# Tiles moved to 128-byte multiples, and another order of work between attention output and FFN, in a one-core diffusion layer

## The chip, the cores and the metric

The kernel runs on one core of a Trainium2 chip. The metric is the device time of one execution in microseconds (us). The core has five engines that work side by side from queues of their own: TensorE (PE in the profile; PEld is its loading of the standing operand), VectorE (DVE), ScalarE (ACT), GpSimd (POOL) and SyncE (SP), which here only issues transfers. A matmul multiplies a *standing* operand of 128 by 128, which is loaded first, with a *moving* operand of 128 partitions by up to 512 columns that streams past it; both are read from SBUF, the on-chip memory of 128 partitions, and the product goes to PSUM.

## The reference

One layer over 256 latent tokens with 256 context tokens, model width 2048, all in float32:

```python
h  = modulate(rms_norm(x, g_attn_pre), sh1, sc1)        # sh, sc, gt: six rows of silu(c) @ w_mod + b_mod
hc = modulate(rms_norm(ctx, g_attn_pre), csh1, csc1)
qa, ka, va, qb, kb, vb, ga, gb = split(h @ w_in)        # the same for hc: keys and values only
oa = window_gqa_latent(rope(qa), rope(ka), va, ka_c, va_c, sink_a)     # 8 heads, 2 key heads
ob = neighbourhood_latent(qb, kb, vb, kb_c, vb_c, rpb_b)               # 8 heads
y  = (sigmoid(ga) * (oa @ w_br_a) + sigmoid(gb) * (ob @ w_br_b)) @ w_o
x  = x + gt1 * rms_norm(y, g_attn_post)
h  = modulate(rms_norm(x, g_ffn_pre), sh2, sc2)
u  = depthwise_conv(h @ w_up)                           # 2 x 5632 channels, 3 taps over tokens
a, g = split(u)
x  = x + gt2 * rms_norm((silu(g) * a) @ w_down, g_ffn_post)
```

## The kernel before

**Arithmetic.** The large products are computed in float32r with both operands split in two: a rounded part (called wh for weights) and the rest (wl). Three products of the four are kept. A weight block is 128 x 2048 floats, 1 MB. `raw_block` loads it into one of four `raw` buffers, `halves` splits it: ACT copies raw to wh (L118), DVE writes raw minus wh to wl (L122), each in two pieces of 1024 columns. wh and wl have two buffers each in pool `wp`. Activations hold rounded part and rest side by side: `hx[:, k, 0]` and `hx[:, k, 1]`, 256 tokens each.

**Two patterns of matmul.** In the first, weights stand and activations move (`mm2`, L164 and L165): for each of the 16 slices of the width there is a pair, wh against 512 columns (rounded part and rest of the activations) and wl against 256 columns (rounded part alone). Queries (pq), gates (pg), branches (pb, moving tile `oab`) and the up projection (pu, moving tile `h2`) are made so. The keys (pk, L387) too, with 256 columns at a time. In the second, activations stand and weights move, in triples: (rounded, wh), (rest, wh), (rounded, wl). The values' projection V (pv, L585, standing `hx`, `hc`), the attention output Wo (py_o, L800, standing `zz`) and the down projection (py_d, L800, standing `ff`) are made so. Attention itself has scores (s, L681, standing q, moving k, 512 columns), transposes (L702) and values (po, L711, standing v, moving `pT`).

**Blocks and their order.** All weight blocks but the first ones stand in one list in order of use: V, queries, gates with branches, Wo (16 blocks), up (88), down (44). `block(ahead, split)` hands out the next one, splits the one after it if `split` is set, and loads `ahead` blocks beyond. The names `queue[...]` and `tc.issue_after(...)` tie a split or another operation to a place behind a given instruction of its engine. Outside one hand-ordered part at the start (keys), a planner orders each engine's queue by priority in the order of the program.

**Where tiles lie.** Pools are stacked from the left end of a partition (byte 16512, a multiple of 128) and from its right end (byte 229344, 96 more than a multiple of 128), in the order in which they are opened and their tiles made. In `cp`, the first tile is `col`, 2080 bytes long, so everything after it starts 32 bytes after a multiple of 128: `raw`, wh and wl too. Small tiles move the rest: hx, h2 and hc start at remainder 64, oab at 32, zz and ff at 96, q, k and v at 0, pT at 96.

**The passage.** `norm_gain` computes Wo (and later down) for 4 column slices of 512 and 2 halves of the tokens (t = 0 and 1). `close(t)` squares the finished slice on ACT with a sum (L805) and multiplies it by the gain row on DVE (L806). In the last slice the order changes: the last `lead` blocks (3 for Wo) are used for all of t = 0 first, then for t = 1, so that the first 128 tokens are done earlier. `done(t)` is here `residual(t)`: the inverse root of the mean square (`rstd_tok`, L836 to L839), the residual sum on DVE (L874) with squares on ACT (L877) for the second norm, its root; and after t = 1 the scaling of both halves (`scaled`, L890 on ACT, L892 on DVE, alternating). The last Wo block is split into buffers of its own in pool `yp` (`place`). The first up block is split between the two halves (`split_to(nblk[0])` after `done(0)`), behind the first residual slice (`queue[b0 + B_UP]`). Then 33 filler matmuls (`keep_busy`, L231) and the transposes of the 16 slices (L905) follow; from their result DVE and ACT make `h2`: a float32 copy h2t (L912 or L914), the rounded part h on ACT (L915), the rest on DVE (L916). With the first slices of h2 the up projection starts, four accumulators at once.

Of the kernel before, what the change touches and what calls it, by code (L numbers as in the profile page):

```python
# [58 lines left out]
def layer_kernel(ctx, tc, xc, xt, ccol, crow, wm_sc, wm_sd, wm_sh, wm_b, cols, wk, wkt, ws, rope, mask_a, bias_b, out):  # L59
# [6 lines left out]
    ps = ctx.enter_context(tc.tile_pool(name="ps", bufs=1, space=bass.MemoryType.PSUM))  # L66

    def acc(name):
        return ps.tile([P, 512], F32, tag="a", bufs=6, name=name)

    def bank(name):
        return ps.tile([P, 512], F32, tag="b", bufs=2, name=name)


    col = cp.tile([P, NCOL], F32, name="col")
    cc = cp.tile([P, KT, 32], F32, name="cc")
# [3 lines left out]
    gcol = cp.tile([P, 2, KT], F32, name="gcol")  # L80
    bgc = cp.tile([P, KT], F32, name="bgc")
    eps = cp.tile([P, 1], F32, name="eps")
    nc.gpsimd.memset(cc, 0.0)
# [6 lines left out]
        out=sel[:], in_=ident[:].rearrange("p (j w) -> p w j", j=4)[:, 0:2, :], axis=mybir.AxisListType.X, op=ALU.add)  # L90
    cr = cp.tile([2 * KT, P], F32, name="cr")
    c2 = cp.tile([P, KT, 2], F32, name="c2")
    nc.scalar.dma_start(out=c2, in_=ccol)
    nc.scalar.activation(cc[:, :, 0:2], c2[:], AF.Silu)

# [43 lines left out]
    raws, parts, nblk, place, queue, last = {}, {q: None for q in range(b0)}, [b0], {}, {}, []  # L139

    def load_to(i):
        for q in range(min(i, len(srcs) - 1) + 1):
            if q not in raws:
                raws[q] = raw_block(*srcs[q])

    def split_to(i):
        load_to(i)
        for q in range(min(i, len(srcs) - 1) + 1):
            if q not in parts:
                parts[q] = halves(raws[q], place.get(q), queue.get(q))  # L150

# [45 lines left out]
    def silu_row(pool, tag="crb", bufs=1, v=0, like=F32):  # L197
        r = pool.tile([P, D], like, tag=tag, bufs=bufs, name=f"crb{v}_{nmod[0]}")
        r = r if like == F32 else r.bitcast(F32)
# [3 lines left out]
    def warm_sqrt(src, nm):  # L203

        t = up.tile([P, 1], F32, tag="warm", bufs=1, name=f"warm_{nm}")
        nc.scalar.activation(t[:], src, AF.Sqrt)

    def gain_cols(i, j0, g0, pool):

        g = pool.tile([P, KT], F32, tag="gr", bufs=1, name=f"gr{i}")  # L210
        nc.vector.tensor_tensor(
            out=g[:], in0=modx[:, j0 : j0 + KT], in1=col[:, C_BMOD + 32 + j0 : C_BMOD + 32 + j0 + KT], op=ALU.add)
        nc.vector.tensor_tensor(out=g[:], in0=g[:], in1=col[:, g0 : g0 + KT], op=ALU.mult)
        return g

    def gain_dram(i, g):

        pt = bank(f"ptg{i}")
        nc.tensor.transpose(pt[:KT, :P], g[:], ident[:])
# [15 lines left out]
    with ExitStack() as mx:  # L235
# [3 lines left out]
        with ExitStack() as at:  # L239
# [162 lines left out]
            for k in range(KT):  # L402
                if k % 2 == 0:
# [7 lines left out]
                    else:  # L411
                        sync.dma_start(out=col[:, C_CW:], in_=cols[:, C_CW:])
                if k == 2:
                    sync.dma_start(out=cr, in_=crow)
                    nc.scalar.activation(cr[:], cr[:], AF.Silu)
                    sync.dma_start(out=sild, in_=cr)
# [254 lines left out]
            def scores(hd):  # L671
# [112 lines left out]

    closed = []

    def norm_gain(act, nk, yg, grow, ss, nm, lead, done, extra=None):


        for c in range(4):  # L790
# [12 lines left out]

            def close(t):
                closed[:] = [nc.scalar.activation(yg[:, t, cs], py[t][:], AF.Square, accum_out=ss[:, t, c : c + 1]).ins]  # L805
                nc.vector.tensor_tensor(out=yg[:, t, cs], in0=py[t][:], in1=grow[:, cs], op=ALU.mult)  # L806
# [8 lines left out]
            if c < 3:  # L815
                for t in range(2):
                    close(t)
                if c == 1:
                    warm_sqrt(ss[:, 0, 0:1], nm)
            else:  # L820
                wts = []
                for g in range(n - lead, n):
                    wts.append(block(3, g < n - 1))
                    part(wts[-1], g, 0)
                for t in range(2):
                    if t:
                        for i, g in enumerate(range(n - lead, n)):
                            part(wts[i], g, 1)
                    close(t)
                    done(t)  # L830
                    if t == 0:
                        split_to(nblk[0])

# [11 lines left out]
    with ExitStack() as ys:  # L845
# [17 lines left out]
        ss = yp.tile([P, 2, 2, 4], F32, name="ss")  # L863
        r = yp.tile([P, 2, 2], F32, name="r")

# [4 lines left out]
        def residual(t):  # L870
            rstd_tok(ss[:, 0, t], r[:, 0, t : t + 1])
            for c in range(4):
                cs = slice(c * 512, c * 512 + 512)
                v_ = nc.vector.scalar_tensor_tensor(  # L874
                    out=x1[:, t, cs], in0=yg[:, t, cs], scalar=r[:, 0, t : t + 1], in1=x1[:, t, cs],
                    op0=ALU.mult, op1=ALU.add)
                a_ = nc.scalar.activation(yg[:, t, cs], x1[:, t, cs], AF.Square, accum_out=ss[:, 1, t, c : c + 1])  # L877
# [8 lines left out]
        def scaled(t):  # L886
            for c in range(4):
                cs = slice(c * 512, c * 512 + 512)
                if c % 2:
                    nc.scalar.activation(yg[:, t, cs], x1[:, t, cs], AF.Copy, scale=r[:, 1, t : t + 1])  # L890
                else:
                    nc.vector.tensor_scalar(  # L892
                        out=yg[:, t, cs], in0=x1[:, t, cs], scalar1=r[:, 1, t : t + 1], scalar2=None, op0=ALU.mult)
            sync.dma_start(out=x1d[:, t], in_=x1[:, t])

        norm_gain(zz, KT, yg, grow, ss[:, 0], "o", 3, residual, beside)
        zs.close()
        pu = [acc(f"pu0_{i}") for i in range(4)]
        keep_busy(33, "2")
        for b in range(8):  # L900
            pt = (acc if b % 2 else bank)(f"ptx{b}")
            for f in range(2):
                for t in range(2):
                    o_ = (2 * b + f) * P
                    nc.tensor.transpose(pt[:, f * S + t * P : f * S + t * P + P], yg[:, t, o_ : o_ + P], ident[:])  # L905
            for f in range(2):
# [4 lines left out]
                if j % 2:  # L911
                    nc.scalar.activation(t_[:], px, AF.Identity, scale=g_, bias=s_)  # L912
                else:
                    nc.vector.tensor_scalar(out=t_[:], in0=px, scalar1=g_, scalar2=s_, op0=ALU.mult, op1=ALU.add)  # L914
                a_ = nc.scalar.activation(h2[:, j, 0], px, AF.Identity, scale=g_, bias=s_)  # L915
# [216 lines left out]
```

## Time and profile before

| | |
|---|---|
| median of 3 runs | 1532.22 us (1531.57 to 1532.34) |
| the profiled execution | 1532.26 us, of which its span 1530.5 us |
| granted clock of TensorE, mean | 0.999 of full speed |
| TensorE matmuls | 9062, busy 1512.7 us |
| keys, until 158 us | DMA at 0.80 to 0.94 of its time |
| V 158 to 275, attention 275 to 440, gates and branches 440 to 691 us | TensorE busy throughout |
| Wo 691 to 780.6 us, passage 780.6 to 791.6 us | in the passage 9.3 of 11.0 us busy, most of it fillers |
| up 791.6 to 1281 us, down 1281 to 1522.5 us | TensorE busy throughout |

Lines of the profile name line of the kernel, engine, operation, result <- operands, shapes and count; then busy time, mean duration in ns, and what the engine waited for before it. A matmul's duration overlaps the next one's, since matmuls are pipelined.

### The profile page before, as it was taken

To read this page: it belongs to the slowest core of one execution; us is meant where nothing else is said; L and a number is where in the kernel's file an instruction comes from. 1 tells how busy PE (TensorE), PEld (TensorE's weight loads), DVE (VectorE), ACT (ScalarE), POOL (GpSimd) and SP (SyncE) were. 2 spreads that over 40 slices of the span, in tenths; PEclk is the share of its full clock that TensorE was granted. 3 is DMA by queue.
4 is the path that set the end of the run, shared out by engine and by line. 5 is a ranking of instruction groups with operands and counts; after the bars stand their busy time and mean duration, and the time that the engine had idled before them with its cause. 6 is when DMAs were issued, how large, how long until landed. Compare 5 with 4: busy or idle time off the path is not lost.

```text
span 1530.5 us, 22661 instructions
## 1 busy us (share of the span) xinstructions
PE 1512.7 (99%) x9062; PEld 1319.4 (86%) x9062; DVE 1131.6 (74%) x1670; ACT 784.7 (51%) x1277; POOL 1.7 (0%) x10
## 2 busy tenths in 40 slices
PE   8999999999999999999999999999999999999998
PEld 8988888899988888888888888888888888888886
DVE  3478798888888989887768887888788776444444
ACT  4332533676774445454467555555555555344342
POOL 0000000000000000000000000000000000000000
PEclk9999999999999999999999999999999999999999
DMA  9978778634458888888955666666666556555552
GB/s 348 385 269 330 287 287 330 256 111 131 139 199 332 320 325 330 336 321 318 376 203 202 248 226 242 245 233 223 242 242 240 198 193 248 220 192 193 192 192 83
DMA packets 59113, 382.19 MB, mean 250 GB/s; under 512 B 6528, under 2 KB 6912, under 8 KB 16768
## 3 DMA queue, kind: packets, MB, share of 16 engines
q1 hardware_dynamic: 58288, 379.68, 67.1%
q8 instruction: 71, 1.16, 0.3%
q10 hardware_dynamic: 720, 1.07, 0.2%
q14 instruction: 34, 0.28, 0.0%
HBM read 376.48 MB, written 4.24 MB: 249 GB/s over the span
## 4 chain that ended last, share of the span: by engine, by line
PE 96%; DVE 1%; ACT 1%; DMA 1%; issue 1%; DVEq 0%; ACTq 0%
PE pu L164 21%; PE py_d L800 16%; PE pu L165 11%; PE pv L585 7%; PE pg L164 7%; PE pk L387 6%; PE py_o L800 5%; PE pq L164 4%; PE pb L164 4%; PE pg L165 4%; PE pq L165 2%; PE pb L165 2%; PE po L711 2%; PE s L681 1%; PE pm L295 1%; PE pt L702 1%
## 5 line engine op out<-in xcount | busy, mean ns | idle before, releaser
L122 DVE TENSOR_TENSOR wl<-raw,wh 128x1024 fp32r<-128x1024 f32 x444 | 529.7, 1221 | 236.7 <-ACT wh L118 236.3
L118 ACT ACTIVATE wh<-raw 128x1024 fp32r<-128x1024 f32 x444 | 453.1, 1054 | 300.8 <-PE py_d L800 131.3
L164 PE MATMUL pu<-h,wh 128*128 128x512 f32 x1408 | 488.6, 390 | 0.1
L165 PE MATMUL pu<-h,wl 128*128 128x256 f32 x1408 | 397.0, 282 | 0.0
L164 PEld LDWEIGHTS pu<-h,wh 128*128 128x128 f32 x1408 | 264.4, 188 | 55.8 <-DVE h L916 0.3
L165 PEld LDWEIGHTS pu<-h,wl 128*128 128x128 f32 x1408 | 266.1, 189 | 0.0
L800 PE MATMUL py_d<-wh,ff 128*128 128x512 f32 x704 | 218.1, 391 | 0.0
L164 PE MATMUL pg<-hx,wh 128*128 128x512 f32 x464 | 161.5, 390 | 0.0
L800 PEld LDWEIGHTS py_d<-wh,ff 128*128 128x128 f32 x704 | 132.2, 188 | 27.9
L194 DVE SCALAR_TENSOR_TENSOR raw<-raw,crb 128x2048 f32<-128x2048 f32 x64 | 146.1, 2285 | 3.8 <-DMA raw<-in_wm_b_dram 3.1
L800 PE MATMUL py_d<-wl,ff 128*128 128x512 f32 x352 | 138.0, 392 | 0.0
L165 PE MATMUL pg<-hx,wl 128*128 128x256 f32 x464 | 130.8, 282 | 0.0
L387 PE MATMUL pk<-hx,ku 128*128 128x256 f32 x480 | 117.0, 286 | 1.8 <-DVE kT L453 1.7
L387 PE MATMUL pk<-hc,ku 128*128 128x256 f32 x480 | 114.1, 280 | 0.0
L169 ACT ACTIVATE half_u<-pu 128x256 f32<-128x256 f32 x88 | 33.5, 383 | 152.8 <-PE pu L165 152.8
L164 PE MATMUL pq<-hx,wh 128*128 128x512 f32 x304 | 108.2, 395 | 0.0
L164 PEld LDWEIGHTS pg<-hx,wh 128*128 128x128 f32 x464 | 87.1, 188 | 18.4
L387 PEld LDWEIGHTS pk<-hx,ku 128*128 128x128 f32 x480 | 90.2, 188 | 6.8 <-issue 4.5
L387 PEld LDWEIGHTS pk<-hc,ku 128*128 128x128 f32 x480 | 90.4, 188 | 0.7 <-issue 0.2
L164 PE MATMUL pb<-oab,wh 128*128 128x512 f32 x256 | 90.5, 394 | 0.0
L165 PEld LDWEIGHTS pg<-hx,wl 128*128 128x128 f32 x464 | 87.7, 189 | 0.0
L165 PE MATMUL pq<-hx,wl 128*128 128x256 f32 x304 | 85.5, 281 | 0.0
(181 smaller groups left out, 1942.5 us busy)
## 6 DMA issues: line engine op xcount, KB each, us to landing
raw<-in_ws_dram SPq DMA_DIRECT2D x222, 1024.0 KB, 4.9
raw<-in_wm_b_dram SPq DMA_DIRECT2D x64, 1024.0 KB, 5.1
raw<-in_wm_sc_dram SPq DMA_DIRECT2D x15, 1024.0 KB, 8.2
raw<-in_wm_sh_dram SPq DMA_DIRECT2D x16, 768.0 KB, 7.2
raw<-in_wkt_dram SPq DMA_DIRECT2D x10, 1024.0 KB, 5.2
crb<-sild SPq DMA_DIRECT2D x6, 1024.0 KB, 7.1
raw<-in_wk_dram SPq DMA_DIRECT2D x7, 768.0 KB, 9.0
sd<-in_wm_sd_dram SPq DMA_DIRECT2D x4, 1024.0 KB, 8.8
```

Source lines behind the costliest of these rows:

```text
L118: a_ = nc.scalar.activation(hi, src, AF.Copy)
L122: v_ = nc.vector.tensor_tensor(out=lo, in0=src, in1=hi, op=ALU.subtract)
L164: nc.tensor.matmul(pt[:, :], wh[:, w], a, start=first and i == 0, stop=False, skip_group_check=True)
L165: nc.tensor.matmul(pt[:, :S], wl[:, w], a[:, 0], start=False, stop=last and i == n - 1, skip_group_check=True)
L169: a_ = nc.scalar.activation(t[:], pt[:, S:], AF.Copy)
L194: nc.vector.scalar_tensor_tensor(out=r, in0=r, scalar=1.0, in1=row, op0=ALU.mult, op1=ALU.mult, accum_out=modx[:, j : j + 1])
L295: nc.tensor.matmul(pm[32 * j : 32 * j + 32, t * P : t * P + P], cc[:, q, :], rsc[k + t][:, q * P : q * P + P], start=q < 4, stop=q >= KT - ...
L387: nc.tensor.matmul(pk[:, v * S : v * S + S], wt[:, w], hh[v][:, k, a], start=k == 0 and a == 0 and wt is wh and v == 0, stop=k == KT - 1 a ...
L585: nc.tensor.matmul(pv[i][:, :nw], src[:, k, a, t0 : t0 + P], wt[:, w], start=k == 0 and q == 0, stop=k == KT - 1 and q == 2)
L681: nc.tensor.matmul(s_ps[:], qs[hd][:, a, qt * P : qt * P + P], k_[:], start=q == 0, stop=q == 2)
L711: nc.tensor.matmul(po[:, :S], v_[:, b], pTs[hd][:, b, a], start=b == 0 and q == 0, stop=b == 3 and q == 2)
L800: nc.tensor.matmul(py[t][:], act[:, k, a, t * P : t * P + P], wt[:, w], start=k == 0 and q == 0, stop=k == nk - 1 and q == 2)
```

## The change

**Addresses.** The tiles of `cp` are put in another order and their sizes chosen so that every large tile starts at a multiple of 128 bytes: `col` goes behind the tiles that matmuls read, the small tiles c2 and cr are dropped (c2 becomes a part of `col` that is filled later, cr uses the buffer of `sd`), a tile `warm` of 96 bytes takes the place of a 4-byte one, `st` gets a fourth buffer, and a tile of 96 bytes (`rim`) is put at the right end. wh and wl buffers grow from 2048 to 2080 floats. `offset` tells where in it a block starts: at 0 where the block moves (V, Wo, down), 8 floats (32 bytes) further on where it stands (keys, queries, gates, branches, up).

**Passage.** `lead` goes from 3 to 2, and the last Wo blocks call for the split of their follower like the others, so that the first up block is split before the first tokens close; the split between the halves is gone. `close(1)` puts its square behind the last square of `residual(0)`. The scaling is ordered anew: first three slices of t = 0 on DVE, then the root for t = 1, then slices (1,0) and (1,2) on DVE, (1,1), (0,3) and (1,3) on ACT. The writes of x1d come last. There are 26 fillers for 33, and the first slice is transposed twice, into two PSUM banks, so that DVE reads one (h2t) and ACT the other (h).

```diff
+    edge = ctx.enter_context(tc.tile_pool(name="edge", bufs=1, side="right"))
+    edge.tile([P, 24], F32, name="rim")
...
-    col = cp.tile([P, NCOL], F32, name="col")
     cc = cp.tile([P, KT, 32], F32, name="cc")
...
     bgc = cp.tile([P, KT], F32, name="bgc")
+    col = cp.tile([P, NCOL], F32, name="col")
...
-    cr = cp.tile([2 * KT, P], F32, name="cr")
-    c2 = cp.tile([P, KT, 2], F32, name="c2")
+    c2 = col[:, C_CW : C_CW + 2 * KT].rearrange("p (k v) -> p k v", v=2)
+    warm = cp.tile([P, 24], F32, name="warm")
...
-    def halves(r, pool=None, after=None):
+    def halves(r, off, pool=None, after=None):
...
-        h = (pool or wp).tile([P, 2048], F32R, tag="wh", bufs=b, name=f"wh{nraw[0]}")
-        lo = (pool or wp).tile([P, 2048], F32R, tag="wl", bufs=b, name=f"wl{nraw[0]}")
+        h, lo = (
+            (pool or wp).tile([P, 2048 + 32], F32R, tag=f"w{q}", bufs=b, name=f"w{q}{nraw[0]}")[:, off[i] : off[i] + 2048]
+            for i, q in enumerate("hl"))
...
+    def offset(i):
+
+        return (0, 0) if i < B_Q or B_WO <= i < B_UP or i >= B_DN else (8, 8)
...
-                h = wp.tile([P, 2048], F32R, tag="wh", bufs=2, name=f"ku{u}")
+                h = wp.tile([P, 2048 + 32], F32R, tag="wh", bufs=2, name=f"ku{u}")[:, 8 : 8 + 2048]
...
+                    cr = sp.tile([P, D], F32, tag="sd", bufs=1, name="cr")[: 2 * KT, :P]
...
-                st_ = at2.tile([P, 2, 4], F32, tag="st", bufs=3, name=f"st{hd}")
+                st_ = at2.tile([P, 2, 4], F32, tag="st", bufs=4, name=f"st{hd}")
...
-                wts = []
+                wts, after = [], None
                 for g in range(n - lead, n):
-                    wts.append(block(3, g < n - 1))
+                    wts.append(block(3))
                     part(wts[-1], g, 0)
...
-                    close(t)
-                    done(t)
-                    if t == 0:
-                        split_to(nblk[0])
+                    close(t, after)
+                    after = done(t)
...
-                if t == c == 0:
-                    queue[b0 + B_UP] = (a_.ins, v_.ins)
-            rstd_tok(ss[:, 1, t], r[:, 1, t : t + 1])
-            if t:
-                with tc.issue_after(closed[0]), tc.issue_after(v_.ins):
-                    scaled(0)
-                scaled(1)
...
+            if t == 0:
+                rstd_tok(ss[:, 1, t], r[:, 1, t : t + 1])
+                return a_.ins
+            else:
+                v_ = v_.ins
+                for c in range(3):
+                    with tc.issue_after(v_):
+                        v_ = scaled(0, c)
+                with tc.issue_after(v_):
+                    rstd_tok(ss[:, 1, t], r[:, 1, t : t + 1])
+                scaled(1, 0)
+                a_ = scaled(1, 1)
+                scaled(1, 2)
+                with tc.issue_after(a_):
+                    a_ = scaled(0, 3)
+                with tc.issue_after(a_):
+                    scaled(1, 3)
+                for q in range(2):
+                    sync.dma_start(out=x1d[:, q], in_=x1[:, q])
...
-        norm_gain(zz, KT, yg, grow, ss[:, 0], "o", 3, residual, beside)
+        norm_gain(zz, KT, yg, grow, ss[:, 0], "o", 2, residual, beside)
...
-        keep_busy(33, "2")
+        keep_busy(26, "2")
...
+        pt0 = acc("ptx0b")
...
-                for t in range(2):
-                    o_ = (2 * b + f) * P
-                    nc.tensor.transpose(pt[:, f * S + t * P : f * S + t * P + P], yg[:, t, o_ : o_ + P], ident[:])
+                turned(pt, 2 * b + f, f * S)
+                if b == f == 0:
+                    turned(pt0, 0, 0)
...
-                    nc.vector.tensor_scalar(out=t_[:], in0=px, scalar1=g_, scalar2=s_, op0=ALU.mult, op1=ALU.add)
+                    nc.vector.tensor_scalar(out=t_[:], in0=px if j else pt0[:, :S], scalar1=g_, scalar2=s_, op0=ALU.mult, op1=ALU.add)
```

More of the change, by code (lines that the diff above doesn't have):

```diff
@@ L90, in layer_kernel @@
         out=sel[:], in_=ident[:].rearrange("p (j w) -> p w j", j=4)[:, 0:2, :], axis=mybir.AxisListType.X, op=ALU.add)
-    cr = cp.tile([2 * KT, P], F32, name="cr")
-    c2 = cp.tile([P, KT, 2], F32, name="c2")
+    c2 = col[:, C_CW : C_CW + 2 * KT].rearrange("p (k v) -> p k v", v=2)
+    warm = cp.tile([P, 24], F32, name="warm")
     nc.scalar.dma_start(out=c2, in_=ccol)
-    nc.scalar.activation(cc[:, :, 0:2], c2[:], AF.Silu)
+    nc.scalar.activation(cc[:, :, 0:2], c2, AF.Silu)
     x1d = tc.dram_tile([P, 2, D], F32, name="x1d")
@@ L149, in split_to @@
             if q not in parts:
-                parts[q] = halves(raws[q], place.get(q), queue.get(q))
+                parts[q] = halves(raws[q], offset(q - b0), place.get(q), queue.get(q))
     def block(ahead=2, split=True):
@@ L197, in silu_row, with warm_sqrt @@
     def silu_row(pool, tag="crb", bufs=1, v=0, like=F32):
-        r = pool.tile([P, D], like, tag=tag, bufs=bufs, name=f"crb{v}_{nmod[0]}")
-        r = r if like == F32 else r.bitcast(F32)
+        r = pool.tile([P, D + (0 if like == F32 else 32)], like, tag=tag, bufs=bufs, name=f"crb{v}_{nmod[0]}")
+        r = r if like == F32 else r[:, :D].bitcast(F32)
         sync.dma_start(out=r, in_=sild[v * KT : v * KT + KT].rearrange("a b -> (a b)").partition_broadcast(P))
         return r
-    def warm_sqrt(src, nm):
-        t = up.tile([P, 1], F32, tag="warm", bufs=1, name=f"warm_{nm}")
-        nc.scalar.activation(t[:], src, AF.Sqrt)
+    def warm_sqrt(src):
+        nc.scalar.activation(warm[:, 0:1], src, AF.Sqrt)
     def gain_cols(i, j0, g0, pool):
-        g = pool.tile([P, KT], F32, tag="gr", bufs=1, name=f"gr{i}")
+        g = pool.tile([P, 2 * KT], F32, tag="gr", bufs=1, name=f"gr{i}")[:, :KT]
         nc.vector.tensor_tensor(
-            out=g[:], in0=modx[:, j0 : j0 + KT], in1=col[:, C_BMOD + 32 + j0 : C_BMOD + 32 + j0 + KT], op=ALU.add)
-        nc.vector.tensor_tensor(out=g[:], in0=g[:], in1=col[:, g0 : g0 + KT], op=ALU.mult)
+            out=g, in0=modx[:, j0 : j0 + KT], in1=col[:, C_BMOD + 32 + j0 : C_BMOD + 32 + j0 + KT], op=ALU.add)
+        nc.vector.tensor_tensor(out=g, in0=g, in1=col[:, g0 : g0 + KT], op=ALU.mult)
         return g
@@ L218, in gain_dram @@
         pt = bank(f"ptg{i}")
-        nc.tensor.transpose(pt[:KT, :P], g[:], ident[:])
+        nc.tensor.transpose(pt[:KT, :P], g, ident[:])
         e = up.tile([P, P], F32, tag="half", bufs=2, name=f"ge{i}")
@@ L413, in layer_kernel @@
                 if k == 2:
+                    cr = sp.tile([P, D], F32, tag="sd", bufs=1, name="cr")[: 2 * KT, :P]
                     sync.dma_start(out=cr, in_=crow)
-                    nc.scalar.activation(cr[:], cr[:], AF.Silu)
+                    nc.scalar.activation(cr, cr, AF.Silu)
                     sync.dma_start(out=sild, in_=cr)
@@ L783, in layer_kernel @@
         br.close()
-    closed = []
     def norm_gain(act, nk, yg, grow, ss, nm, lead, done, extra=None):
@@ L802, in part, with close @@
                             start=k == 0 and q == 0, stop=k == nk - 1 and q == 2)
-            def close(t):
-                closed[:] = [nc.scalar.activation(yg[:, t, cs], py[t][:], AF.Square, accum_out=ss[:, t, c : c + 1]).ins]
+            def close(t, after=None):
+                with ExitStack() as es:
+                    if after:
+                        es.enter_context(tc.issue_after(after))
+                    nc.scalar.activation(yg[:, t, cs], py[t][:], AF.Square, accum_out=ss[:, t, c : c + 1])
                 nc.vector.tensor_tensor(out=yg[:, t, cs], in0=py[t][:], in1=grow[:, cs], op=ALU.mult)
@@ L818, in norm_gain @@
                 if c == 1:
-                    warm_sqrt(ss[:, 0, 0:1], nm)
+                    warm_sqrt(ss[:, 0, 0:1])
             else:
-                wts = []
+                wts, after = [], None
                 for g in range(n - lead, n):
-                    wts.append(block(3, g < n - 1))
+                    wts.append(block(3))
                     part(wts[-1], g, 0)
@@ L863, in layer_kernel @@
         ss = yp.tile([P, 2, 2, 4], F32, name="ss")
-        r = yp.tile([P, 2, 2], F32, name="r")
+        r = yp.tile([P, 2, 8], F32, name="r")
         crb = silu_row(yp)
@@ L877, in residual @@
                 a_ = nc.scalar.activation(yg[:, t, cs], x1[:, t, cs], AF.Square, accum_out=ss[:, 1, t, c : c + 1])
-                if t == c == 0:
-                    queue[b0 + B_UP] = (a_.ins, v_.ins)
-            rstd_tok(ss[:, 1, t], r[:, 1, t : t + 1])
-            if t:
-                with tc.issue_after(closed[0]), tc.issue_after(v_.ins):
-                    scaled(0)
-                scaled(1)
[L886 to L894, printed above, removed]
@@ L897, in layer_kernel, with scaled @@
+        def scaled(t, c):
+            cs = slice(c * 512, c * 512 + 512)
+            if c == 3 or (t, c) == (1, 1):
+                return nc.scalar.activation(yg[:, t, cs], x1[:, t, cs], AF.Copy, scale=r[:, 1, t : t + 1]).ins
+            return nc.vector.tensor_scalar(
+                out=yg[:, t, cs], in0=x1[:, t, cs], scalar1=r[:, 1, t : t + 1], scalar2=None, op0=ALU.mult).ins
+        norm_gain(zz, KT, yg, grow, ss[:, 0], "o", 2, residual, beside)
         zs.close()
         pu = [acc(f"pu0_{i}") for i in range(4)]
-        keep_busy(33, "2")
+        keep_busy(26, "2")
@@ L900, in layer_kernel, with turned @@
+        def turned(pt, j, o):
+            for t in range(2):
+                nc.tensor.transpose(pt[:, o + t * P : o + t * P + P], yg[:, t, j * P : j * P + P], ident[:])
+        pt0 = acc("ptx0b")
         for b in range(8):
```

## The prediction

> **What bounds the kernel now.** I read the page's busy times and its chain first, then the groups of matmuls with shapes kept apart, then the stretches by stage, and last the chain inside the passage from the attention output into the FFN.
>
> ```profile
> span 1530.5 us, 22661 instructions
> PE 1512.7 (99%) x9062; PEld 1319.4 (86%) x9062; DVE 1131.6 (74%) x1670; ACT 784.7 (51%) x1277; POOL 1.7 (0%) x10
> PE 96%; DVE 1%; ACT 1%; DMA 1%; issue 1%; DVEq 0%; ACTq 0%
> ```
>
> The matmul engine is busy for 99% of the span and holds 96% of the chain that ends last. So two things can move the end: how long one matmul occupies the engine, and the few microseconds in which the chain leaves it. The profiled execution took 1532.26 us, 1.76 us more than its span; the median of the runs is 1532.22 us. I add to 1532.26.
>
> A matmul's printed duration overlaps the next one, so I need the distance between starts. In the up projection (timeline of the engine):
>
> ```profile
> 1000.01 0.28 PE L165 MATMUL pu<-h,wl 128*128 128x256 f32 x1
> ...
> 1003.82 0.28 PE L165 MATMUL pu<-h,wl 128*128 128x256 f32 x1
> ```
>
> There are eleven pairs (512 columns with the rounded part wh, 256 columns with the rest wl) between these starts: 3.81/11 = 0.346 us a pair, while the printed durations add to 0.672 us. Each printed duration therefore has about 163 ns of overlap (half of 0.672 - 0.346). What I use is differences of durations, taking the overlap as equal for equal widths. The groups by shape (last columns: busy us, mean ns of one):
>
> ```profile
> L164 PE MATMUL pu<-h,wh 128*128 128x512 f32 x1408 | 488.6, 390 | 0.1
> L165 PE MATMUL pu<-h,wl 128*128 128x256 f32 x1408 | 397.0, 282 | 0.0
> L800 PE MATMUL py_d<-wh,ff 128*128 128x512 f32 x704 | 218.1, 391 | 0.0
> L164 PE MATMUL pg<-hx,wh 128*128 128x512 f32 x464 | 161.5, 390 | 0.0
> L164 PE MATMUL pq<-hx,wh 128*128 128x512 f32 x304 | 108.2, 395 | 0.0
> L164 PE MATMUL pb<-oab,wh 128*128 128x512 f32 x256 | 90.5, 394 | 0.0
> L800 PE MATMUL py_o<-wh,zz 128*128 128x512 f32 x256 | 79.0, 392 | 0.0
> L585 PE MATMUL pv<-wh,hc 128*128 128x512 f32 x128 | 40.3, 396 | 0.0
> ```
>
> One and the same operation, 512 columns after a load of 128 by 128, costs 390 ns in one stage and 396 in another. The attention scores (timing of one source line, shortest/median/longest) are shorter than either:
>
> ```profile
> L681 PE MATMUL s<-k,q x96: 387/389/499, 286.1 to 424.2; 128*128 128x512 f32 x96
> L711 PE MATMUL po<-pT,v x192: 277/281/387, 301.7 to 440.2; 128*128 128x256 f32 x192
> L387 PE MATMUL pk<-hc,ku x480: 274/280/390, 10.7 to 163.5; 128*128 128x256 f32 x160
> ```
>
> By the order and sizes of the tiles, scores are the one wide stage whose two operands start at multiples of 128 bytes. Written as moving/standing remainder of 128, the others are: up, gates, queries and keys 64/32, branches 32/32, V 32/64, Wo and down 32/96, values 96/0. That an address matters, not only the loop, shows inside Wo: its last weight block lies in a buffer of its own pool. The same groups in the window 692 to 746 us, and in 777.8 to 780.6 us, where only that block runs:
>
> ```profile
> L800 PE MATMUL py_o<-wh,zz 128*128 128x512 f32 x158 | 49.0, 391 | 0.0
> L800 PE MATMUL py_o<-wh,zz 128*128 128x512 f32 x8 | 2.5, 396 | 0.0
> ```
>
> Same loop, same activations, another weight buffer: 5 ns more. Both buffers have remainder 32 of 128, so 128 bytes can't be the whole rule; this is the weakest point of what follows.
>
> **Part 1, the addresses.** No instruction is added; tiles move. Afterwards the moving operand has remainder 0 everywhere, and the standing one 32 where weights stand (keys, queries, gates, branches, up) and 0 in V, Wo, down, scores and values. For 0/0 the scores are a true row: 389 ns. For 0/32 there is no row. Bounds for the wide matmul of a pair are 387 ns (the shortest of the scores) and 396 (V); for its 256-column partner 274 (shortest of the keys) and 282 or a little more. I take 389, the only row with a moving operand at a multiple of 128, and 281 for the partner, the median of the values, whose standing operand is aligned.
>
> - Down: the 704 with wh and, at the same price, the half as many with wl, 1056 x 2 ns = 2.1 us. Wo likewise 384 x 3 = 1.2 us. V, for both inputs and both parts, 384 x 7 = 2.7 us. Sum 6.0 us.
> - Up and gates: (1408 + 464) x 1 ns = 1.9 us. Queries the same 1 ns, 0.3 us: their mean of 395 holds waits behind transposes, which stay. Branches: 256 x 5 ns = 1.3 us.
> - The 256-column partner: (1408 + 464 + 304 + 256) x 1 ns = 2.4 us.
> - Keys: 0. Their stage has the DMA engines as a second limit, and a shorter matmul would wait there:
>
> ```profile
> 12.00:100.00 88.00, 84.77 (x1058) 80.86 (x1057) 45.31 (x81) 38.37 (x66) 0.00 (x0) 1.00 0.94 357
> 440.00:691.00 251.00, 251.00 (x1445) 221.54 (x1444) 221.41 (x292) 129.11 (x214) 0.00 (x0) 1.00 0.84 319
> ```
>
> (Columns: span, busy PE, PEld, DVE, ACT, POOL, granted clock, DMA share, GB/s.) At a share of 0.94 in DMA I credit nothing, with 960 x 2 ns = 1.9 us either way as its bound. In the gates and branches DVE is busy 221.41 of 251 us; it would bound only if that stage shrank by some 30 us, and I ask about 3. The clock is 1.00, so it has nothing to give. Part 1 sums to 6.0 + 3.5 + 2.4 = 11.9 us.
>
> Edits at nothing: the conditioning tile inside col, cr in the buffer of sd, four st buffers, the rim, the wider tiles. c2 and the first columns of col are different columns; were they ordered all the same, col's load would wait for the first Silu, with the first x and weights behind it on SP. I price that only as a tail of the chances.
>
> **Part 2, the passage.** The chain of waits from the last square of the first 128 tokens to the first up matmul:
>
> ```profile
> 779.72 1.72 ACT yg L877 x5
> 781.47 1.05 ACT wh L118
> 782.54 1.12 DVE wl L122
> ...
> 784.53 2.74 DVE x L874 x4
> 787.27 0.40 DVE yg L892
> ...
> 788.28 0.30 ACT r L838
> ...
> 789.94 0.56 DVE h2t L914
> 790.52 0.57 ACT h L915
> ...
> 791.60 0.51 PE pu L164
> ```
>
> The split of the first FFN block (wh L118, wl L122) lies in this chain. With lead 2 instead of 3, the block before the last two is used up before the first tokens close, its buffer comes free, and the split runs earlier. Rows of the timeline from there on:
>
> ```profile
> 775.74 0.60 ACT L805 ACTIVATE yg<-py_o 128x512 f32<-128x512 f32 x1 [7.82 <-PE py_o L800]
> 776.46 0.69 DVE L806 TENSOR_TENSOR yg<-py_o,grow 128x512 f32<-128x512 f32 x1 [6.72 <-ACT yg L805]
> 777.26 2.74 DVE L874 SCALAR_TENSOR_TENSOR x<-yg,r,x 128x512 f32<-128x512 f32 x4
> 780.64 0.38 PE L231 MATMUL busy<-ident,ones 128*128 128x128 f32 x2
> 782.60 0.57 ACT L805 ACTIVATE yg<-py_o 128x512 f32<-128x512 f32 x1
> 788.81 1.33 ACT L890 ACTIVATE yg<-x,r 128x512 f32<-128x512 f32 x2 [0.23 <-DVE r L839]
> ```
>
> The Wo matmuls end at 780.64 us, where the fillers start; 10.96 us pass until the first up matmul. Before the first tokens' close ACT idles 7.82 us and DVE 6.72, against the split's two halves of 1.05 and 1.12 us each. If that cover fails (buffer or raw block late), the split stays in the chain and the gain is nil.
>
> What is late next: the Square of the second tokens (782.60) has to wait, by the new order, for the last square of the first ones, near 780.7 (L874 ends at 780.0, a square takes some 0.7); its root, and DVE's product with grow, stand behind it. From Square to the first L874 the first tokens needed 775.74 to 777.26 = 1.5 us, without a split between; the second ones took 782.60 to 784.53. So L874 starts near 782.4 to 782.8, about 1.9 us earlier. Against it: three instead of two scalings of the first tokens (0.40 each) stand on DVE ahead of the sums for the second norm, and those wait for the third, while before they slipped in behind the first: 787.27 to 788.28 becomes 1.5 us, +0.5. The copy of the first transposes in its own bank lets ACT's h start beside DVE's h2t: -0.56, +0.2 for two more transposes; but ACT now has three scalings there (two took 1.33 us), which can push h back by 0.7: about +0.2 together. Sum -1.9 + 0.5 + 0.2, rounded to **-1.2 us** (bounds -2.2 and +1). Seven fillers fewer cost nothing: they only fill this wait. Both x1d writes now queue on SP behind the scalings, and weight loads no longer behind the first of them; x1d is read back only after the FFN. After the first up matmul the engine runs without a gap, so what is gained at the start stays.
>
> **Forecast:** 1532.26 - 11.9 - 1.2 = 1519.2, say **1519 us**.
>
> **Rivals.**
> 1. *The distance decides, not the remainder* (slower). The one stage whose standing operand lies 32 beyond the moving one is V, 396 ns; that is just what queries, gates and up get. Then (1408 + 464 + 304) x 6 = +13.1 us, branches 256 x 2 = +0.5, the 0/0 stages keep -6.0, the passage -1.2: 1538.7, say **1539 us**. For it: the Wo buffers above, which differ by 128 but not in the remainder of 128. Against: V has triples, not pairs, and a moving remainder of 32. It decides from a mean of 393 ns in pu L164 and its like: 3 ns x 2432 pairs eat the 7.2 us of the rest.
> 2. *Addresses don't matter*; the differences come from the loops and the passage alone changes: **1531 us**. For it: pairs, triples and lone shapes differ as much as addresses do. Against: the 391 and 396 of Wo. [...]
> 3. *All excess goes*: wide matmuls reach 387 and narrow 274, the shortest seen. Pairs: (1408 + 464 + 304) x 3 + 256 x 7 + 2432 x 8 = 27.8 us; triples: another 2 ns x 1440 = 2.9 on 6.0; with the passage 37.9: **1494 us**. For it: the narrow ones leave 274 only now and then. Against: a short one follows a long one there, so the minimum is no mean.
>
> **Chances.** Forecast 0.43 (its own range 1510 to 1527); rival 1 0.17; rival 2 0.17; rival 3 0.16; even shorter than 1490 0.03; the passage or the start lost on top of no gain 0.04. A measurement of this kernel tells a change from none at about 0.2%, 3 us. Faster: 0.43 + 0.16 + 0.03 = 0.62; same: rival 2 and half of the last, 0.19; slower: 0.19. The range goes from 1494 (half of rival 3 below) to 1540 (rival 1 with half of the keys' 1.9 us): some 0.15 is left out.
>
> **What would show it.** Means of pu L164 and pg L164: 389 or less for the forecast, 393 and more for rival 1, 390 for rival 2. pv at 389 instead of 396 and py_d at 389 carry the surest half. pu L165 at 281, or near 275 for rival 3. In the passage: no wh L118 between 776 us and the first pu, and 9.8 us from the first filler to the first pu. I am wrong if the interval per pair moves by over 6 ns either way, or if the chain goes to DVE in the gates.

## The result and the profile after

The changed kernel takes 1542.05 us (median of 6 runs, 1541.74 to 1542.40), the kernel before, run beside it, 1531.89 us (6 runs, 1531.47 to 1532.34). The ratio is 1.0066 with a 95% interval of 1.0053 to 1.0079: 10 us **slower**, where 13 us faster was forecast, and 2 us beyond the end of the range.

The page of the changed kernel: span, busy times, chain by engine.

```profile
span 1540.4 us, 22638 instructions
PE 1523.3 (99%) x9050; PEld 1315.9 (85%) x9050; DVE 1132.7 (74%) x1671; ACT 782.5 (51%) x1276; POOL 1.7 (0%) x10
...
PE 96%; DMA 2%; DVE 1%; ACT 0%; issue 0%; SPq 0%; DVEq 0%; ACTq 0%
```

Nothing new bounds it: PE is as full as before and still holds 96% of the chain. PE itself is busy 10.6 us longer, with twelve fewer instructions. The groups of its matmuls by shape (busy us, mean ns of one):

```profile
L175 PE MATMUL pu<-h,wh 128*128 128x512 f32 x1408 | 495.1, 395 | 0.0
L176 PE MATMUL pu<-h,wl 128*128 128x256 f32 x1408 | 394.3, 280 | 0.0
L809 PE MATMUL py_d<-wh,ff 128*128 128x512 f32 x704 | 219.0, 392 | 0.0
...
L175 PE MATMUL pg<-hx,wh 128*128 128x512 f32 x464 | 163.7, 395 | 0.0
...
L175 PE MATMUL pb<-oab,wh 128*128 128x512 f32 x256 | 90.7, 395 | 0.0
...
L809 PE MATMUL py_o<-wh,zz 128*128 128x512 f32 x256 | 79.3, 393 | 0.0
...
L596 PE MATMUL pv<-wh,hc 128*128 128x512 f32 x128 | 39.8, 392 | 0.0
```

The wide matmul of up and gates went from 390 to 395 ns, the value above 393 that the prediction gave to its first rival. Down and Wo went up by 1 each instead of down by 2 and 3; only V fell, 396 to 392, by 4 of the 7 ns that were expected.

Printed durations overlap, so I measure each stage between starts: from its first matmul to the first of the next stage (down and Wo: to their last). Up, for example, runs from the first to the second of these rows (timeline of PE), 496.0 us; in the kernel before it ended at the third.

```profile
793.98 0.50 PE L175 MATMUL pu<-h,wh 128*128 128x512 f32 x1
...
1289.98 0.62 PE L809 MATMUL py_d<-wh,ff 128*128 128x512 f32 x2
```

```profile
1281.04 0.63 PE L800 MATMUL py_d<-wh,ff 128*128 128x512 f32 x2
```

| stage, us | before | after | difference |
|---|---|---|---|
| up to the first key matmul | 10.3 | 9.7 | -0.6 |
| keys | 147.8 | 149.1 | +1.3 |
| V | 117.0 | 116.0 | -1.0 |
| queries and attention | 165.3 | 166.6 | +1.3 |
| gates and branches | 250.9 | 253.1 | +2.2 |
| Wo | 89.2 | 89.6 | +0.4 |
| last Wo matmul to first up matmul | 11.2 | 9.7 | -1.5 |
| up | 489.4 | 496.0 | +6.6 |
| down | 241.5 | 242.8 | +1.3 |

The differences add to 10.0 us. The passage gains what it should; nearly everything else with a matmul in it loses, up most.

Now follow up block by block. These are the starts of four weight blocks, 16 pairs each, in the changed kernel's timeline:

```profile
856.84 0.39 PE L175 MATMUL pu<-h,wh 128*128 128x512 f32 x1
...
862.49 0.39 PE L175 MATMUL pu<-h,wh 128*128 128x512 f32 x1
...
868.09 0.39 PE L175 MATMUL pu<-h,wh 128*128 128x512 f32 x1
...
873.74 0.39 PE L175 MATMUL pu<-h,wh 128*128 128x512 f32 x1
```

They are 5.65, 5.60 and 5.65 us apart: 353, 350, 353 ns a pair, in turn. In the kernel before, whole blocks took 346.7, all but two near the end; these two starts are 5.55 us apart:

```profile
870.47 0.39 PE L164 MATMUL pu<-h,wh 128*128 128x512 f32 x1
...
876.02 0.39 PE L164 MATMUL pu<-h,wh 128*128 128x512 f32 x1
```

Down does the same in the changed kernel, with 24 matmuls a block:

```profile
1289.98 0.62 PE L809 MATMUL py_d<-wh,ff 128*128 128x512 f32 x2
...
1295.42 0.62 PE L809 MATMUL py_d<-wh,ff 128*128 128x512 f32 x2
...
1301.02 0.63 PE L809 MATMUL py_d<-wh,ff 128*128 128x512 f32 x2
...
1306.47 0.62 PE L809 MATMUL py_d<-wh,ff 128*128 128x512 f32 x2
```

5.44, 5.60 and 5.45 us: 227, 233, 227 ns a matmul. Two buffers serve such a ring in turn, and with 2048 + 32 floats a buffer is 8320 bytes long, 32.5 times 256. A period of 128 bytes doesn't fit the two Wo buffers of the kernel before, with 391 and 396 ns at one remainder of 128, so I try 256: then every second block lies half a period away from the others. This alternation is the lead for the experiments. **Distance** below means: the start of the standing operand that is loaded next, minus the start of the moving operand that streams meanwhile, modulo 256 bytes. By the tiles' addresses:

| distance (ns per pair or matmul) | before | after, two blocks in turn |
|---|---|---|
| up, gates (pairs) | 224 (346.7) | 32 (353.0), 160 (349.9) |
| branches (pairs) | 128 (350.9) | 32 (353.0), 160 (350.0) |
| V (triples, 512 columns) | 32 (233.4) | 0 (227.1), 128 (233.2) |
| Wo, down (triples) | 192 (228.9) | 0 (227.3), 128 (233.0) |

**The theory** (D in the expectations, A in experiment 5) is that the distance modulo 256 alone sets the interval between matmuls. **Its rivals:** the passage, or the order of work it brings, does harm further on; addresses don't matter (rival 2 of the prediction); or another distance would bring the matmuls down to the shortest durations seen, 387 and 274 ns (rival 3), so that the kernel before was no better than a chance point.

### The profile page after: what moved, and what is told of

Same layout as the page of the kernel before. It is cut to its first block, busy times and chain, and to the rows that moved or that the text cites. A ratio compares the mean times of both kernels' runs of the same rounds, so it can differ in the third digit from the quotient of the medians.

```text
span 1540.4 us, 22638 instructions
## 1 busy us (share of the span) xinstructions
PE 1523.3 (99%) x9050; PEld 1315.9 (85%) x9050; DVE 1132.7 (74%) x1671; ACT 782.5 (51%) x1276; POOL 1.7 (0%) x10
## 4 chain that ended last, share of the span: by engine, by line
PE 96%; DMA 2%; DVE 1%; ACT 0%; issue 0%; SPq 0%; DVEq 0%; ACTq 0%
PE pu L175 21%; PE py_d L809 16%; PE pu L176 11%; PE pv L596 7%; PE pg L175 7%; PE pk L397 6%; PE py_o L809 6%; PE pq L175 4%; PE pb L175 4%; PE pg L176 4%; PE pq L176 2%; PE pb L176 2%; PE po L722 1%; PE s L692 1%; PE pt L713 1%; PE pm L305 1%
## 5 line engine op out<-in xcount | busy, mean ns | idle before, releaser
L128 DVE TENSOR_TENSOR wl<-raw,wh 128x1024 fp32r<-128x1024 f32 x444 | 529.3, 1221 | 239.7 <-ACT wh L124 239.1
L175 PE MATMUL pu<-h,wh 128*128 128x512 f32 x1408 | 495.1, 395 | 0.0
```

The lines of the kernel that those rows point to most:

```text
L128: v_ = nc.vector.tensor_tensor(out=lo, in0=src, in1=hi, op=ALU.subtract)
L175: nc.tensor.matmul(pt[:, :], wh[:, w], a, start=first and i == 0, stop=False, skip_group_check=True)
```

## The experiments

**1. Each half of the change alone.** passage_alone is the kernel before with the new order of the passage only; addresses_alone is the changed kernel with the old passage.

```diff
 passage_alone, against the kernel before
-                    wts.append(block(3, g < n - 1))
+                    wts.append(block(3))
...
-        norm_gain(zz, KT, yg, grow, ss[:, 0], "o", 3, residual, beside)
+        norm_gain(zz, KT, yg, grow, ss[:, 0], "o", 2, residual, beside)
```

> The kernel before with only the new passage (lead 2, no split between the halves, scaling anew, first slice transposed twice, 26 fillers); all tiles stay where they were. Theory A (the slowdown is all in the addresses, the passage gains what it gained in the changed kernel): 1.5 us less than before, 1530.4 us, with 9.7 instead of 11.2 us from the last Wo matmul to the first up matmul. Rival (the passage moved work into other stages and cost time there): 1532 us or more.

> The changed kernel with the passage of before put back; only the addresses are new. Theory A: 11.7 us more than before, 1543.6 us, pu L175 near 395 ns. Rival (half of the loss comes from the new passage and its order of work): 1537 us.

passage_alone: 1530.57 us (10 runs), ratio 0.9990 [0.9980, 0.9999]. addresses_alone: 1543.40 us, ratio 1.0074 [1.0059, 1.0089]. Against the 1531.99 us of the kernel before in the same series that is -1.4 and +11.4 us, together +10.0, next to +10.2 for the whole change. Up takes 489.4 us with the new passage and the old addresses, 496.1 with the reverse. So the passage does no harm further on. The chain of waits of passage_alone, in order of time (start, length, what):

```profile
781.16 0.20 ACT yg L806
...
781.39 0.40 DVE yg L807
...
782.25 2.74 DVE x L873 x4
784.98 1.19 DVE yg L901 x3
...
786.52 0.30 ACT r L837
...
787.59 0.33 PE ptx L911
...
789.99 0.46 PE pu L164
```

The split of the first FFN block, which stood between the last square and the product with grow, is gone from the chain. DVE's sums for the residual (L873) start 1.8 us after the first filler (which starts at 780.47 here); before it was 3.9 us (780.64 to 784.53). Of these 2.1 us some are given back: three scalings (L901, 1.19 us) now stand where one did.

**2. Another distance, the same for all blocks.** further_224 makes the buffers 2112 floats wide (8448 bytes, 33 times 256), so both of a ring have one distance, and puts the standing weights of all pairs, and the keys', at 224, where those of all but the branches were before; V, down and Wo (but for its last block) go to 0. The offsets of 56 and, for the branches, 24 floats both give 224, because their moving operands start at different places.

```diff
 further_224, against the changed kernel
-            (pool or wp).tile([P, 2048 + 32], F32R, tag=f"w{q}", ...)[:, off[i] : off[i] + 2048]
+            (pool or wp).tile([P, 2048 + 64], F32R, tag=f"w{q}", ...)[:, off[i] : off[i] + 2048]
...
-        return (0, 0) if i < B_Q or B_WO <= i < B_UP or i >= B_DN else (8, 8)
+        if i < B_Q or B_WO <= i < B_UP or i >= B_DN:
+            return 0, 0
+        if i < B_UP and (i >= B_WO - 3 or (i >= B_BR + 6 and (i - B_BR) % 3 == 0)):
+            return (24, 24)
+        return (56, 56)
```

> The changed kernel with wh and wl buffers of 2112 floats (a multiple of 256 bytes) for 2080, so that both buffers of a ring start alike, and with standing weights 224 bytes beyond the moving operand, counted round 256, in place of 32; where weights move, the distance is 0 round 256, but for the last Wo block. Eps, sel and the warm cell share a tile and Gc lies in gcol, for room. Theory D (what counts is the distance from the moving to the standing start, modulo 256): pairs return to before (pu 390 and 282 ns), V, Wo and down go to 389; with the passage 1524 to 1526 us. Rival M (a moving start at a multiple of 128 is itself bad): stays near 1542. Rival R (the remainder of the standing start modulo 128 counts, 96 is as 224): no number, but pv and py would not change from the changed kernel, 392 to 393 ns.

1524.25 us (1524.13 to 1524.62), ratio 0.9950 [0.9933, 0.9967]: faster than both kernels. Its groups by shape:

```profile
L178 PE MATMUL pu<-h,wh 128*128 128x512 f32 x1408 | 488.5, 390 | 0.0
L179 PE MATMUL pu<-h,wl 128*128 128x256 f32 x1408 | 396.9, 282 | 0.0
L812 PE MATMUL py_d<-wh,ff 128*128 128x512 f32 x704 | 216.5, 389 | 0.0
L178 PE MATMUL pg<-hx,wh 128*128 128x512 f32 x464 | 161.5, 390 | 0.0
...
L599 PE MATMUL pv<-wh,hc 128*128 128x512 f32 x128 | 39.4, 389 | 0.0
```

Up and gates are back at 390 and 282, and the triples of V and down at 389, what the prediction had for them. Down takes 239.1 us, -2.4 against before, V 114.8, -2.2, gates and branches 249.8, -1.1, since the branches come from 128 to 224. V's last slice, 256 columns wide, goes the other way: 119.9 ns a matmul at distance 0, where it took 118.2 at 32. The moving operands of the pairs still start at multiples of 128, so that remainder is not what counted. For the pairs of up there is nothing beyond this: 346.7 ns, as before.

**3. One distance changed in the kernel before.** rim_192 adds one unused tile of 192 bytes at the right end of the memory. It moves the activations that stand in Wo and down from 192 to 0 (in Wo's last block from 64 to 128), and those that move in the branches from 128 to 64; no instruction changes.

```diff
 rim_192, against the kernel before
+    edge = ctx.enter_context(tc.tile_pool(name="edge", bufs=1, side="right"))
+    edge.tile([P, 48], F32, name="rim")
```

> The kernel before, with one unused tile of 192 bytes at the right end of each partition, and nothing else: zz and ff, which stand in Wo and down, come from distance 192 to 0 round 256 behind wh and wl; oab comes from distance 128 to 64; queries, gates, up, keys and V keep their distances. Theory D with the distance map (227.4 ns a matmul at 0, 229.2 at 192): 1.8 ns x (1056 + 360) = 2.5 us less, given back in part in the branches (352.9 for 350.3 ns a pair, +0.7 us): 1530.2 us. Rival M (remainders of 128): Wo and down stay at remainder 32 moving, no change, 1532.

1529.64 us (11 runs), ratio 0.9985 [0.9976, 0.9994]. Down takes 239.1 us, -2.4, Wo 88.4, -0.8; gates and branches 251.4, +0.5, since the branches' pairs grew from 350.9 to 352.3 ns. Its group for down:

```profile
L802 PE MATMUL py_d<-wh,ff 128*128 128x512 f32 x704 | 216.8, 389 | 0.0
```

**4. Maps.** further_224 with a distance that goes on from block to block, in steps of 32 bytes (distance_map) or 16 (finer_map). In distance_map the two parts of a pair step separately through 64 combinations. Each map ran once (1534.53 and 1535.27 us) and is used for its trace alone.

```diff
 distance_map, against further_224 (finer_map: 4 * (... % 16), and d, d in up too)
+        if i >= B_DN:
+            d = 8 * ((i - B_DN) % 8)
+            return d, d
+        if i >= B_UP + 4:
+            n = i - B_UP - 4
+            return 8 * (n % 8), 8 * (n // 8 % 8)
```

> The same kernel, but the up blocks place wh and wl at all 64 combinations of 0, 32, ... 224 bytes beyond h2 (wh runs fastest, 84 blocks of two columns of tiles, 16 pairs each), and the down blocks move from 0, 32, ... 224 bytes, so that ff stands 0, -32, ... behind them. Theory D: pairs with both at 224 take 347 ns, both at 32 353, both at 128 351, both at 160 350; triples at distance 0 take 227 ns a matmul, at 32 233, at 64 234, at 128 233, at 192 229. Rival (modulo 128): 32 and 160 alike, 0 and 128 alike. Rival (addresses don't count): all pairs alike.

> The kernel of further_224, but the up blocks stand at 0, 16, ... 240 bytes beyond h2 (wh and wl alike), the down blocks move from 0, 16, ... 240 bytes, and the 24 weight units of the keys stand at 0, 32, ... 224 bytes. [...]

distance_map's timeline, starts of four blocks of down and of the next, with distances 0, 224, 192, 160:

```profile
1324.53 0.63 PE L818 MATMUL py_d<-wh,ff 128*128 128x512 f32 x2
...
1329.99 0.63 PE L818 MATMUL py_d<-wh,ff 128*128 128x512 f32 x2
...
1335.60 0.63 PE L818 MATMUL py_d<-wh,ff 128*128 128x512 f32 x2
...
1341.10 0.63 PE L818 MATMUL py_d<-wh,ff 128*128 128x512 f32 x2
...
1346.71 0.63 PE L818 MATMUL py_d<-wh,ff 128*128 128x512 f32 x2
```

5.46, 5.61, 5.50 and 5.61 us for 24 matmuls: 227.5, 233.8, 229.2, 233.8 ns. Means of both maps over whole blocks, from the starts in the traces (ns a matmul in down's blocks, ns a pair in up's; for the pairs of distance_map the block with both parts at the distance, for those of finer_map the later turns of the cycle):

```
distance            0     32    64    96    128   160   192   224
triples, map       227.6 233.2 233.5 234.1 233.3 233.8 229.4 233.5
triples, finer     228.4 232.9 233.0 233.8 232.7 233.9 229.4 233.5
pairs, map         353.2 353.2 352.6 347.2 351.0 350.3 353.3 346.9
pairs, finer       346.6 346.8 352.8 347.4 350.9 349.9 353.3 346.8
```

Triples agree with the theory in every column to about 1 ns, and with the kernels above to 2: 0 is best, 192 next, the rest 4 to 7 ns worse. The finer map's steps between fill in one more good place, 16 (227.0); 144, 176 and 240 lie in the middle, near 231. Pairs agree from 64 to 224, but at 0 and 32 the two maps differ by 6 to 7 ns. What finer_map was to say of the keys can't be read from it: of the three units at distance 0 one took 119.9 ns a matmul on average and the others 177 and 182, waits included. In the finer map even the blocks of one distance differ. These are starts of a block at 224, one at 0, one at 16, and then, a turn later, of a block at 240, one at 0, one at 16:

```profile
804.72 0.39 PE L184 MATMUL pu<-h,wh 128*128 128x512 f32 x1
...
810.27 0.40 PE L184 MATMUL pu<-h,wh 128*128 128x512 f32 x1
...
815.92 0.40 PE L184 MATMUL pu<-h,wh 128*128 128x512 f32 x1
...
894.31 0.39 PE L184 MATMUL pu<-h,wh 128*128 128x512 f32 x1
...
899.96 0.39 PE L184 MATMUL pu<-h,wh 128*128 128x512 f32 x1
...
905.50 0.40 PE L184 MATMUL pu<-h,wh 128*128 128x512 f32 x1
```

The first block at 0, entered from a block at 224, took 5.65 us, 353 ns a pair. The second, entered from 240, took 5.54, 346 ns, and so did the four later ones. So the theory is too simple for pairs. A new one, theory B in the expectations below: a distance allows one or two steady rhythms, and the block before decides which is kept.

**5. All pairs at one doubtful distance.** all_at_32 and all_at_0 are further_224 with 32 or 0 in place of 224. If a rhythm is kept, all blocks of up must have the same one.

```diff
 all_at_32 (all_at_0: 32, 32 and 0, 0), against further_224
-            return (24, 24)
-        return (56, 56)
+            return (40, 40)
+        return (8, 8)
```

> The kernel of further_224 with one number changed: every standing weight 32 bytes beyond its moving operand modulo 256 instead of 224, the same for both buffers of each ring (wh, wl, ku, the branches too). V, Wo and down stay at 0. Theory A (the distance alone sets the interval): a pair takes 353 ns, as the changed kernel's blocks at 32 and the first map's 32/32 block do, so up is 489.4 + 1408 x 6.3 ns = 498.3 us and the whole 1524.3 + 2432 x 6.3 ns = 1539.6 us. Theory B (a block keeps one of two rhythms, and the block before it decides which: in finer_map the blocks at 32 take 346.8 ns, entered from a block at 16): all blocks being alike now, there is no alternation that throws them out; either the whole of up stays on 347 (up 489 to 490 us, whole 1524 to 1526 us) or the whole on 353 (as A). 350 on average, with blocks that alternate, would speak against both.

> The same with distance 0 in all pairs: standing and moving operand start at the same remainder of 256. Theory A takes the value of the first map's block at 0/0, 353 ns: up 498.3 us, whole 1539.6 us. Theory B knows two rhythms at 0 as well: finer_map's first block at 0, entered from blocks at 224, took 353.3 ns, and each later one, entered from 240, 346.6 ns. So up lies at 489 to 490 or at 498 us, the same in every block, and the whole at 1524 to 1526 or near 1539 us. If distance 0 were as plainly best for pairs as it is for triples (227.4 ns, the lowest), it would be 1524 or less.

> further_224 once more, for its spread. all_at_32 and all_at_0 took two times each from one program and one set of addresses (1528 to 1531 and 1537 to 1540 us; 1529 and 1539 us), as two rhythms would give that an execution falls into by chance. If 224 is a distance with one rhythm only, as in before (19 executions within 1.0 us), every execution of this lies between 1524.0 and 1525.5 us. If it has a second rhythm as well, some of the executions lie 5 to 16 us higher, and the 7.7 us gained before were luck.

Three consecutive blocks of up start at these times, first in all_at_32, then in all_at_0:

```profile
855.84 0.40 PE L178 MATMUL pu<-h,wh 128*128 128x512 f32 x1
...
861.49 0.40 PE L178 MATMUL pu<-h,wh 128*128 128x512 f32 x1
...
867.14 0.40 PE L178 MATMUL pu<-h,wh 128*128 128x512 f32 x1
```

```profile
853.41 0.39 PE L178 MATMUL pu<-h,wh 128*128 128x512 f32 x1
...
858.95 0.39 PE L178 MATMUL pu<-h,wh 128*128 128x512 f32 x1
...
864.50 0.39 PE L178 MATMUL pu<-h,wh 128*128 128x512 f32 x1
```

5.65 us a block at 32 and 5.55 at 0. It stays so over 81 whole blocks in a row, 353.3 and 346.7 ns a pair within 0.1 ns: in up, where moving tile and distance stay the same, a rhythm once entered is kept. A buffer is 8448 bytes long here, 33 times 256, and successive blocks take the same time within 0.01 us; with 8320, 32.5 times 256, they took 5.65 and 5.60 in turn. Distance 0 has both rhythms within one execution, as the groups of all_at_0 show:

```profile
L178 PE MATMUL pu<-h,wh 128*128 128x512 f32 x1408 | 488.5, 394 | 0.0
L179 PE MATMUL pu<-h,wl 128*128 128x256 f32 x1408 | 390.1, 277 | 0.0
...
L178 PE MATMUL pg<-hx,wh 128*128 128x512 f32 x464 | 164.1, 398 | 0.0
...
L179 PE MATMUL pg<-hx,wl 128*128 128x256 f32 x464 | 130.1, 280 | 0.0
```

Both stages have the same shapes and distance, yet 394 + 277 in up and 398 + 280 in the gates. (Note that 394 alone looks worse than the 390 of the kernel before; the interval, 346.7, is the same. Only starts tell.) Within the gates the rhythm changes: the first three blocks take 346.7 ns a pair, but once a block of the branches has run between, those of the gates take 352.2 and 353.6 in turn, and the branches themselves mostly 347.1. Two successive blocks of the gates, 5.64 us apart:

```profile
462.80 0.40 PE L178 MATMUL pg<-hx,wh 128*128 128x512 f32 x1
...
468.44 0.40 PE L178 MATMUL pg<-hx,wh 128*128 128x512 f32 x1
```

And the executions of one program differ:

| kernel | executions, us |
|---|---|
| all_at_32 | 1528.2; 1530.7, 1531.1, 1531.1; 1537.2; five from 1539.7 to 1540.1 |
| all_at_0 | nine from 1528.8 to 1529.6; 1539.3 |
| further_224, both series | nine from 1523.9 to 1524.8 |
| before, beside all_at_32 and all_at_0 | nineteen from 1531.5 to 1532.5 |

The granted clock of TensorE was 0.998 or 0.999 in every one of these, so it is not what differs. The expectation for all_at_0 (1524 or 1539) missed a mixture: its first queries and most of its gates hold the longer rhythm, or nearly, and up the shorter. Against further_224 its keys take 1.9 us more, queries and attention 0.8, gates and branches 2.7: the 5 us between 1524.2 and 1529.5. The ratios, 1.0025 [1.0005, 1.0045] at 32 and 0.9989 [0.9975, 1.0003] at 0, say mostly how many executions fell on which side. That the quicker executions of all_at_32 are those with up at 347 is argued from the 9 us between 1531 and 1540 (1408 pairs x 6.6 ns = 9.3 us); only one execution, of the upper group, has a trace. If it is so, the rest of the pairs stayed at 353 there, and the expectation, which had 1524 to 1526 or 1540, missed this mixture too. What made 1528.2 and 1537.2 isn't known. further_224_again confirmed the gain: 1524.22 us, ratio 0.9949 [0.9935, 0.9962].

## Why the prediction was wrong

- **What bounds the kernel** was read rightly: the length of the matmuls and the passage; little else moved the end.
- **The step that failed** is the one that priced the 0/32 stages: "I take 389, the only row with a moving operand at a multiple of 128". It took the remainder of 128 as the cause. The runs put the distance modulo 256 in its place: further_224 keeps the moving operands at multiples of 128 and brings the pairs of up from the distances 32 and 160 to 224; they take 346.7 ns instead of 353.0 and 349.9. Up, gates, branches and queries were to give 3.5 us and their partners 2.4; instead up alone lost 6.6. The prediction called this point its weakest (two Wo buffers, 391 against 396, equal modulo 128). They lay at 192 and 64, half of 256 apart, so its own rows spoke for a longer period than 128.
- **Down, Wo and V** were priced right for distance 0: -2.4, -0.8 and -2.2 us in further_224, against -2.1, -1.2 and -2.7. V's -2.2 holds a loss of 0.3 us in its 256-column slice, and Wo's last block stays at 128. What was wrong is that the change would put all of them at 0. The buffer of 8320 bytes put every second block at 128, and the measured sums were +1.3, +0.4 and -1.0.
- **The scores' 389 ns** were no safe price either. Their distance is 0 before and after, yet their median went from 389 to 394 ns, and that of the interval between two of them from 227 to 231. That the entry counts, as with pairs, would fit; it wasn't tried.
- **The 256-column partner** did fall, 282 to 280, as predicted (281), but that was no gain: within a pair one matmul gives what the other takes (390 + 282 in up before and 394 + 277 in all_at_0, both at 346.7 ns a pair). The two durations should not have been priced apart.
- **Keys** at nothing, with 1.9 us either way: +1.3, inside the bound. In addresses_alone, with the keys at the same addresses, it was +0.3, so most of the 1.3 isn't shown to come from the addresses.
- **The passage** was right: no split in the chain, 9.49 us from the first filler (784.49) to the first up matmul (793.98) where 9.8 was forecast, -1.5 us where -1.2 was, and passage_alone gives the same -1.5 by itself. Its terms came true as well: counted from the first filler, the residual's sums start 2.1 us earlier (1.9 forecast), and the three scalings ahead of the root take 0.5 us more (0.5 forecast). The edits at nothing show no cost.
- **Rival 1** was the mechanism, by its own sign: a mean of pu over 393. It ended at 1539 because it kept the 6.0 us of the 0/0 stages, which became a loss of 0.7, while its 6 ns a pair came out as 4.8 in up. Its chance of 0.17 was too low for what its Wo row weighed; the range ended on it with only half a bound added.
- **Rival 2** falls with rim_192: 192 bytes of unused memory alone shorten down by 2.4 us. **Rival 3** falls with the maps: of all distances and combinations tried, no whole block of up, gates or branches has a mean under 346.5 ns a pair, and none of V, Wo or down under 226.6 ns a matmul of 512 columns. The pairs of up and gates in the kernel before were already at the shortest that was seen; only branches, V, Wo and down had something to gain.

## What to carry to other kernels

In this kernel the distance was worth 6 ns a matmul (down after the change: 227.3 at 0, 233.0 at 128). Where matmuls with a fresh standing operand each run back to back, try laying tiles out by the difference of the two operands' starts modulo 256 bytes, with each ring's buffers a multiple of 256 bytes long: buffers of 8320 bytes gave successive blocks of up 353.0 and 349.9 ns a pair, buffers of 8448 at distance 224 gave 346.7. No one distance was best here: 0 for triples of 512 columns (227.6 ns in distance_map, the others 229.4 to 234.1), 224 for pairs (346.7), and in V's triples of 256 columns 32 was better than 0 (118.2 against 119.9). So measure each stream for itself. Measure from start to start over a whole block, for each buffer of the ring apart; the mean duration of a group hides the alternation and can move against the interval (394 in all_at_0 and 390 before, at the same 346.7). For pairs prefer a distance whose executions all agree: 224 gave 1523.9 to 1524.8 us here, 0 gave 1528.8 to 1529.6 and 1539.3, and 32 from 1528.2 to 1540.1.

## What the hardware showed that was not expected

- A matmul of 512 columns takes 227 to 234 ns by the distance alone, with the same operation, shapes and data: 227.6 at distance 0 and 234.1 at 96 in distance_map, 227.3 and 233.0 in turn in the changed kernel's down, at 0 and 128. What in the engine makes the distance count, no run shows.
- A floor remains: at the best distance 226.7 ns for 512 columns, and no distance that was tried brought a whole block under 226.6. What part of this goes with the columns isn't settled: 256 columns took 119.9 ns at distance 0 (V of further_224), 6 more than half of the 227.1 there (V of the changed kernel), and 118.2 at 32, 1.5 more than half of 233.4 (V before).
- A stream of pairs has more than one steady rhythm at some distances (346.7 and 353.3 ns at 0 and 32), keeps the one it enters while moving tile and distance stay the same (81 blocks of up), and one program can take 1528 or 1540 us in different executions. What decides the entry, and whether it is the distance to the operand just loaded or to the one loaded next that counts, stays open: within a block the two are equal.
